# One head's row maxima among the last projections, and VectorE's subtractions at the streams' ends, in a two-layer attention trunk

## The chip, the core and the metric

The kernel runs on one core of one Trainium2 chip. The metric is the device time of one execution in microseconds (us); three runs of the kernel before took 2885.28 to 2890.05 us, with a median of 2886.47 us. TensorE (PE in the profile) multiplies, VectorE (DVE), ScalarE (ACT) and GpSimd (POOL) work on elements, SyncE (SP) issues most loads and stores.

## The reference

The function maps `x` (2048 x 1024, fp32) to an output of the same shape through two layers. Each layer is, in short:

```
hn   = rms_norm(h, norm_pre[i])
proj = hn @ w_in                      # q, k, v (or low-rank parts of them), memory queries, gate
main = 12 causal heads of width 64    # layer A: latent attention with rotary keys
                                      # layer B: logits plus F[t] - F[s], F the cumulative log forget gate
mem_out = 4 heads of cross-attention into 256 memory tokens
y    = concat(main, mem_out) * silu(gate)
h    = h + rms_norm(y @ w_out[i], norm_post[i])
```

Every product is computed at about fp32 precision: an operand is split into a high and a low part, and three products of parts are summed.

## The kernel before

**Stages.** Each layer has projections (layer A: `proj_a`, `up_a`; layer B: `proj_b`, L870 on), an attention stream and `out_proj`. Layer A's `out_proj` and layer B's projections run interleaved. Queries are taken in four groups of 512 (`g`), keys in blocks of 128.

**The stream.** A `Unit` is one head and one group g; a memory unit is one memory head and one group. The stream goes through the units in steps of up to 1024 columns (`flow`): logits on PE (`s_logits`, L1709), exponential on ACT (L1651), its fp16 high part on ACT (`hi`, L202), the low part, exponential minus high part (`lo`, L224), on POOL where the step is wider than 512 columns and else on DVE, then the values on PE (L1725). Before a unit's first step its rows must be there: the maxima of its logits, which PE computes (L1580 for causal units, L1562 for memory units), DVE reduces (L1551; L1583 for the masked block on the diagonal) and PE and DVE write as extra rows beside q (L1600, L1601). In the steady stream the rows of later units stand between the steps of earlier ones.

**The start of layer B's stream.** The last chunk of the projections is run for g = 1, 2, 3, 0. Before g = 3, `att_start` records the memory head, with eight early memory units whole (`run_early`: rows, logits, values) at a higher priority, so that they come between projection matmuls; before g = 0, `att_head` records the loads of head 0's keys and values. Head 0's rows stand at the head of the stream itself.

**q tiles.** A causal unit of layer B needs a q tile of 76 rows (`qb`, four per head, even heads in slot A3, odd ones in A0) and one of 128 rows (`qa`). Of the second kind there are four in slot R1, and four more in another slot (A4) for units after the last memory unit and a few more (`free`).

**out_proj.** For an output tile t of 128 queries, `z_prep` loads the gate and the attention output (L1195, L1196), multiplies them on POOL (L1200), transposes on PE (L1204), and splits; the matmuls are L1229. `z_prep(0)` is recorded behind the loads of two gains.

**What sets the order.** The projections and the early units are ordered by a scheduler with priorities; in the streams every engine follows the order in which the code records, SP too. The buffers are tiles in named slots (A0 to A8, R0 to R4, S, G, Q), which are given out again when their last reader is done, and a load into a slot waits for that on SP with all that is queued behind it.

Of the kernel before, what the change touches and what calls it, by code (L numbers as in the profile page):

```python
# [42 lines left out]
NR = 4  # L43
# [9 lines left out]
MEM_EARLY = {0: 6, 1: 8}  # L53
MEM_FIRST = {0: 4, 1: 4}
# [138 lines left out]
class Trunk:  # L193
    def __init__(self, tc, ins, out):
        self.tc, self.nc, self.i, self.out = tc, tc.nc, ins, out
        self.alt = 0
        self.owed = 0.0

# [663 lines left out]
    def proj_b(self, hn0):  # L862
# [153 lines left out]

    def att_start(self, l):

        nc, B = self.nc, self.box
        if l == 0:  # L1020
# [15 lines left out]
        ap["pm"], ap["ps"], ap["pv"] = self.banks(2, 3), self.banks(5, 6), self.banks(0)  # L1036
        self.l, self.yt = l, {}
# [28 lines left out]
    def att_head(self):  # L1066

        l, B = self.l, self.box
        self.v0 = B("A2" if l == 0 else "A8")
        self.kv_place("0", B("A1" if l == 0 else "A2", r=True), self.v0)  # L1070
# [3 lines left out]
        for _, f, _ in self.head0.prep():  # L1074
            f()

    def attention(self):
        nc, l, ap, B = self.nc, self.l, self.ap, self.box
        nb = DH + FB
# [5 lines left out]
        mb, jb = (v0, yb) if l == 0 else (ap["sp"],) * 2  # L1085
        mqk = self.mqk = mb.tile([P, G], BF16, name="mqk")
        ap["mj"] = Turn(jb.tile([P, G], BF16, name="mj"))
        nc.gpsimd.memset(mqk, 0.0)
        nc.gpsimd.affine_select(out=mqk[:, G - P:G], in_=mqk[:, G - P:G], compare_op=ALU.is_ge, fill=NEG, base=0,
                                pattern=[[-1, P]], channel_multiplier=1)  # L1090
# [5 lines left out]
        if l:  # L1096
            qa = B("R1", r=True)
            ap["qa"] = Turn(*(Later(lambda k=k: qa.tile([P, G], F32R, name=f"qa{k}")) for k in range(4)))
            qb = B("A3", r=True), B("A0", r=True)
            self.qb_t = [qb[j // NG].tile([nb, 2, G], F32R, name=f"qb{j}") for j in range(2 * NG)]  # L1100
            for g in range(NG):
# [693 lines left out]
```

## Time and profile before

| what | value |
|---|---|
| median of 3 runs | 2886.47 us |
| profiled execution, its own time | 2885.39 us |
| its span (first to last instruction) | 2883.7 us |
| PE busy, mean granted clock | 2789.8 us (97%), 0.976 |
| DVE, ACT, POOL busy | 1563.8, 1323.0, 1251.2 us |

The shares are means over stages. The places at which PE is not at its full clock and busy are what the tables below are cut from: the start and the end of each stream, and two short waits within the second one. A granted clock of 1.00 is 2.4 GHz and 0.50 is 1.2 GHz.

### The profile page before, as it was taken

What the parts mean: (1) busy time and instruction counts of PE and PEld (TensorE: products, weight loads), DVE (VectorE), ACT (ScalarE), POOL (GpSimd) and SP (SyncE); (2) the same over time, 40 slices, a digit from 0 to 9 for tenths busy, and PEclk for the clock granted to TensorE, in tenths of its full rate; (3) what the DMA queues carried; (4) which work ended last, traced back from release to release, by engine and by line L of the source; (5) the groups of instructions that cost most, each with busy time, mean ns of one, the idle gap of its engine ahead of it and who ended that gap; (6) DMA issues with size and microseconds to landing.
All of it is one profiled execution on the core that took longest, in us unless ns stands there. A gap on an engine that the chain in (4) does not pass through costs nothing. (4 is left out here: it accounts for less than half of the span.)

```text
span 2883.7 us, 58600 instructions
## 1 busy us (share of the span) xinstructions
PE 2789.8 (97%) x24017; PEld 2379.9 (83%) x24017; DVE 1563.8 (54%) x3358; ACT 1323.0 (46%) x1867; POOL 1251.2 (43%) x838
## 2 busy tenths in 40 slices
PE   7999999879999999999999999999999999999998
PEld 6789998657888888878888997999767788887787
DVE  7522215467777777745463325310268788887343
ACT  4322123237778788852141010111137788888311
POOL 2110123346677777772101002310037788888431
PEclk9999999979999999999999999999979999999999
DMA  5343447763433343255443223861454454465453
GB/s 186 125 140 100 133 146 264 229 204 93 106 74 88 76 100 93 55 190 190 146 156 118 76 82 121 291 225 61 132 149 113 116 134 123 112 171 170 147 175 117
DMA packets 260933, 398.42 MB, mean 138 GB/s; under 512 B 24793, under 2 KB 140521, under 8 KB 260521
## 3 DMA queue, kind: packets, MB, share of 16 engines
q1 hardware_dynamic: 180112, 255.21, 31.4%
q10 hardware_dynamic: 79016, 138.27, 13.3%
q8 instruction: 189, 3.10, 0.5%
q0 software_dynamic: 1536, 1.18, 0.3%
q14 instruction: 80, 0.65, 0.1%
HBM read 238.13 MB, written 156.47 MB: 137 GB/s over the span
## 5 line engine op out<-in xcount | busy, mean ns | idle before, releaser
L224 POOL TENSOR_TENSOR bA<-bA,bA 128x1024 f16<-128x1024 f32 (+5 forms) x277 | 507.8, 1844 | 293.9 <-ACT bA L202 219.5
L255 PE MATMUL banks<-bR,bA 128*128 128x256 f32 (+3 forms) x4437 | 549.1, 286 | 1.1 <-DVE bQ L507 0.6
L255 PEld LDWEIGHTS banks<-bR,bA 128*128 128x128 f32 x4437 | 540.7, 188 | 6.5 <-ACT bG L505 0.9
L255 PE MATMUL banks<-bA,bR 128*128 128x512 f32 (+2 forms) x2208 | 514.6, 390 | 6.9 <-ACT bS L823 4.2
L1709 PE MATMUL banks<-bA,bA 96*128 96x512 f32 (+13 forms) x1820 | 483.9, 377 | 0.3 <-ACT bA L1651 0.2
L255 PEld LDWEIGHTS banks<-bA,bR 128*128 128x128 f32 x2208 | 403.4, 191 | 93.3 <-ACT bS L823 5.4
L1651 ACT ACTIVATE bA<-banks 128x1024 f32<-128x1024 f32 (+1 forms) x414 | 370.7, 895 | 182.9 <-PE banks L1709 156.9
L1551 DVE TENSOR_REDUCE mx<-banks 128x1 f32<-128x512 f32 x576 | 387.8, 685 | 108.3 <-PE banks L1580 105.6
L202 ACT ACTIVATE bA<-bA 128x1024 f16<-128x1024 f32 (+5 forms) x400 | 336.5, 848 | 95.8 <-DMA qrs<-bA 22.0
L1709 PEld LDWEIGHTS banks<-bA,bA 96*128 96x128 f32 (+3 forms) x1820 | 327.5, 193 | 43.1 <-ACT bA L1651 0.9
L1580 PE MATMUL banks<-bA,bA 76*128 76x512 f32 (+5 forms) x868 | 317.3, 406 | 17.6 <-DVE bA L1601 4.9
L209 POOL TENSOR_SCALAR bR<-bR 128x1024 fp32r<-128x1024 f32 (+3 forms) x50 | 61.5, 1230 | 410.8 <-PE banks L255 360.1
L1583 DVE CUSTOM_DVE_ANT_0 bA<-banks,bA 128x128 bf16<-128x128 f32 (+3 forms) x384 | 186.6, 486 | 76.7 <-PE banks L1580 66.1
L1229 PE MATMUL banks<-bA,bA 128*128 128x512 f32 x960 | 226.6, 392 | 0.0
L1725 PEld LDWEIGHTS <-bA 128*128 128x128 f16 x5928 | 198.9, 99 | 28.9 <-issue 16.5
L1229 PEld LDWEIGHTS banks<-bA,bA 128*128 128x128 f32 x960 | 178.6, 188 | 36.1
L1580 PEld LDWEIGHTS banks<-bA,bA 76*128 76x128 f32 (+1 forms) x868 | 164.2, 196 | 50.5 <-DVE bA L1601 7.6
L1709 PE MATMUL banks<-bR,bA 128*128 128x512 f32 (+6 forms) x620 | 201.6, 391 | 0.9 <-DVE bR L1601 0.9
L224 POOL TENSOR_TENSOR bR<-bR,bR 128x1024 f16<-128x1024 f32 (+2 forms) x74 | 159.9, 2161 | 81.7 <-ACT bR L202 49.5
L1200 POOL TENSOR_TENSOR bA<-bA 128x512 f32<-128x512 f32 x64 | 102.4, 1622 | 207.8 <-DMA bA<-gs 195.1
L224 POOL TENSOR_TENSOR bR<-bA,bR 128x1024 f16<-128x1024 f32 (+2 forms) x76 | 154.7, 2038 | 67.4 <-ACT bR L202 31.0
L505 ACT ACTIVATE bG<-banks 128x256 f32<-128x256 f32 x128 | 49.1, 385 | 277.2 <-PE banks L255 197.2
(228 smaller groups left out, 3638.7 us busy)
## 6 DMA issues: line engine op xcount, KB each, us to landing
bA<-qbs SPq DMA_DIRECT2D x65, 256.0 KB
bA<-in_x_dram SPq DMA_DIRECT2D x32, 512.0 KB
gs<-bG ACTq DMA_DIRECT2D x128, 128.0 KB
bA<-gs SPq DMA_DIRECT2D x32, 512.0 KB
bA<-ys SPq DMA_DIRECT2D x32, 512.0 KB
bA<-h SPq DMA_DIRECT2D x28, 512.0 KB
ks<-bA ACTq DMA_DIRECT2D x24, 512.0 KB
qs<-bA ACTq DMA_DIRECT2D x24, 512.0 KB
```

The costliest lines, as they stand in the source:

```text
L202: nc.scalar.activation(out, in_, AF.Copy, scale=scale)
L209: nc.gpsimd.tensor_scalar(out, in_, scale, 0.0, op0=ALU.mult, op1=ALU.add)
L224: e.tensor_tensor(out=out, in0=in_, in1=hi, op=ALU.subtract)
L255: nc.tensor.matmul(out, lhsT=a, rhs=b, start=start and i == 0, stop=stop and i == n - 1)
L1200: nc.gpsimd.tensor_tensor(out=gt[:, hs], in0=gt[:, hs], in1=yt[:, hs], op=ALU.mult)
L1229: nc.tensor.matmul(ps[:, ns], lhsT=a, rhs=b[:, ns], start=c == 0 and j == 0, stop=c == KC - 1 and j == 2)
L1551: nc.vector.tensor_reduce(out=to, in_=ps, axis=AX.X, op=ALU.max, negate=negate)
L1580: nc.tensor.matmul(ps, lhsT=q[0:qr, t * P:(t + 1) * P], rhs=k[0:kr, x:x + w], start=True, stop=True)
L1583: nc.vector.tensor_tensor_reduce(out=ap["mj"].next()[:, 0:w], in0=ps, in1=K.mqk[:, G - w:G], scale=1.0, scalar=-3.0e38, op0=ALU.add, op1=A ...
L1651: nc.scalar.activation(pf[:, 0:w], ps[:, 0:w], AF.Exp, scale=self.scale, bias=LOGP)
L1709: nc.tensor.matmul(ps[:, o:o + bw], lhsT=k[0:kr, (self.k0 + kt) * P:(self.k0 + kt + 1) * P], rhs=q[0:qr, q0:q0 + bw], start=i == 0 and not ...
L1725: nc.tensor.matmul(self.pv[:, t, 0:n], lhsT=p[:, o:o + P], rhs=v[:, kv, a:a + n], start=self.first, stop=False, skip_group_check=True)
```

## The change

Layer B's first causal head and its memory units change places. `att_head` is called before the chunk g = 2, takes head 0's slots (k in A4, v in A5, q rows in A6) and now also records the row maxima of all four of head 0's units, at a priority of its own; `att_start` follows before g = 0. Four early memory units are run whole instead of eight, two more get only their rows (`ready`), and two instead of four stand ahead of head 0 in the stream; further memory units stand behind two groups of each head from head 0 on, so that they last for five heads. The planner counts rows that are there already, and q tiles are loaded ahead at each step. The slots of layer B move: the `qb` tiles of even heads are in A6 and those of odd heads in A3, late `qa` tiles in A7. When all rows of a stream are recorded, `lo` runs on DVE at every width, right behind the step's ACT work. In `out_proj` the first two output tiles are multiplied on DVE, and `z_prep(0)` is recorded ahead of the gains.

```diff
-MEM_EARLY = {0: 6, 1: 8}
-MEM_FIRST = {0: 4, 1: 4}
+ROWS_AHEAD = 600
+MEM_EARLY = {0: 6, 1: 4}
+MEM_READY = {0: 2, 1: 2}
+MEM_FIRST = {0: 4, 1: 2}
...
-            if g == 0:
+            if g == 2:
                 yield
-            elif g == 3:
+                env = (stp, self.banks(4, 7), hn)
+            elif g == 0:
                 yield
-                env = (stp, self.banks(4, 7, 1), hn)
             for k, (_, ms) in enumerate(last):
                 self.run_chunk(env, ms, W[len(jobs) - 2 + k], g)
...
-            km, ph, pa, ymp, qq = B("A4", r=True), B("A5"), B("A7"), B("A1"), B("R4", r=True)
+            km, ph, pa, ymp, qq = B("A7", r=True), B("A1"), B("A2"), B("A8"), B("R4", r=True)
             pl, pfs, vmp, vrp, nrp, sp, qqs = ph, (pa,) * 3, ymp, ymp, pa, pa, (km, km, qq, qq)
...
-        for u in first:
+        ready = self.mem_units[:MEM_READY[l]]
+        for u in first + ready:
             u.q = ap["qq"].next()
         with self.tc.high_priority(offset=EARLY_AHEAD):
-            run_early(mem, first)
+            run_early(mem, first, ready)
 
     def k_ones(self, j):
         k = self.k_t[j]
...
+        self.att_place(l)
+        self.v0 = B("A2" if l == 0 else "A5")
+        self.kv_place("0", B("A1" if l == 0 else "A4", r=True), self.v0)
...
+        self.ready = {}
+        if l == 0:
+            return
+        self.max_mask(self.v0, self.v0)
+        self.qb_t = {}
+        self.qb_place("A6", 0)
+        with self.tc.high_priority(offset=ROWS_AHEAD):
+            for g in range(NG):
+                u = self.ready[g] = Unit(self, l, self.head0, 0, g)
+                u.q_row()
+                for f, _ in u.max_closures():
+                    f()
+                u.nm()
+                u.nm_row()
+
...
+    def qb_place(self, slot, odd):
+
+        nb = DH + FB
+        box = self.box(slot, r=True)
+        for g in range(NG):
+            t = self.qb_t[g + NG * odd] = box.tile([nb, 2, G], F32R, name=f"qb{g}")
+            ind = self.v0.tile([FB, G], F32, name="ind")
+            self.nc.gpsimd.memset(ind, 1.0)
+            for lo_b, hi_b in ((-(NR + 2 * g), 0), (0, NR + 1 + 2 * g)):
+                self.nc.gpsimd.affine_select(out=ind, in_=ind, compare_op=ALU.is_ge, fill=0.0, base=lo_b + hi_b,
+                                             pattern=[[0, G]], channel_multiplier=1 if lo_b else -1)
+            self.nc.vector.tensor_copy(t[DH:nb], ind[:, None, :].to_broadcast([nb - DH, 2, G]))
...
-        self.kv_place("1", B("A3" if l == 0 else "A6", r=True), yb if l == 0 else B("Q"))
+        self.kv_place("1", B("A3" if l == 0 else "A0", r=True), yb if l == 0 else B("Q"))
...
         units = [mu.pop(0) for _ in range(min(MEM_FIRST[l], len(mu)))]
         for h, hd in enumerate(heads):
...
-            late = mid + [later("A4", q1, k) for k in range(4)]
+            late = mid + [later("A7", q1, k) for k in range(4)]
...
-            u.q = min(ts, key=lambda q: used.get(q, -1))
+            u.q = u.q or min(ts, key=lambda q: used.get(q, -1))
...
-        zb, gb, xp = (B("A1", r=True), B("A2"), B("A8")) if l == 0 else (B("A1", r=True), B("A3"), B("A4"))
+        zb, gb, xp = (B("A1", r=True), B("A2"), B("A8")) if l == 0 else (B("A8", r=True), B("A3"), B("A7"))
         sp = self.sm
         pt_, po, npt = self.banks(2, 3), self.banks(4, 6), self.banks(0, 1)
-        gain = xp.tile([P, D], F32, name="ogain")
-        self.bcast_row(gain, i["norm_post"][l])
-        if l == 0:
-            self.xbox = B("A6")
-            gpre = self.gpre = self.xbox.tile([P, D], F32, name="ogpre")
-            self.bcast_row(gpre, i["norm_pre"][1])
-
...
-                nc.gpsimd.tensor_tensor(out=gt[:, hs], in0=gt[:, hs], in1=yt[:, hs], op=ALU.mult)
+                (nc.vector if t < 2 else nc.gpsimd).tensor_tensor(out=gt[:, hs], in0=gt[:, hs], in1=yt[:, hs], op=ALU.mult)
...
         nxt = z_prep(0)
+        gain = xp.tile([P, D], F32, name="ogain")
+        self.bcast_row(gain, i["norm_post"][l])
+        if l == 0:
+            self.xbox = B("A6")
+            gpre = self.gpre = self.xbox.tile([P, D], F32, name="ogpre")
+            self.bcast_row(gpre, i["norm_pre"][1])
...
-    for u in objs[:3]:
+    both = objs + ready
+    for u in both[:3]:
         u.q_dma()
-    for u in objs[:2]:
+    for u in both[:2]:
         rows(u)
     for k, u in enumerate(objs):
-        if k + 3 < len(objs):
-            objs[k + 3].q_dma()
-        if k + 2 < len(objs):
-            rows(objs[k + 2])
+        if k + 3 < len(both):
+            both[k + 3].q_dma()
+        if k + 2 < len(both):
+            rows(both[k + 2])
...
+        if o.has_row:
+            at += sum(c for _, c in o.max_closures())
+            maxq.extend(late)
+            late.clear()
+            continue
...
+        q_ahead(u + 2, u)
         close()
-        todo = advance(u, min(t * rate + lead, RUNUP * (t + 4 * G) + need[0]))
+        todo = advance(u, min(t * rate + lead, RUNUP * (t + 4 * G) + need[0] + done))
...
-        o.flow(s, box)
+        o.flow(s, box, st["k"] == len(maxq) and not todo)
         if before:
             before[0].flow_lo(before[1])
         before = None
+        if st["k"] == len(maxq) and not todo:
+            o.flow_lo(box)
+            box["dve"] = False
...
+    def q_row(self):
+
+        K, h, g = self.K, self.h, self.g
+        if self.mx_ops:
+            return
+        kb, nb = self.hd.kt[1], DH + FB
+        qb = self.qb = K.qb_t[g + NG * (h % 2)]
+        K.load_r(qb[0:DH], K.qbs[h // 2][(h % 2) * DH:(h % 2) * DH + DH, :, g * G:(g + 1) * G])
+        self.mx_ops = ((qb[:, 0], nb), (kb, nb))
+        self.nmrow, self.at = qb[DH:DH + NR, 1], DH
...
+        if self.loaded:
+            return
+        self.loaded = True
         if self.kind == "fox":
-            src = K.qbs[h // 2][r, :, sl]
+            self.q_row()
...
-            K.load_r(qa, src[:, 0].unsqueeze(0).to_broadcast([2, DH, G]))
-            self.mx_ops = ((qb[:, 0], nb), (kb, nb))
-            self.nmrow, self.at = qb[DH:DH + NR, 1], DH
-            self.passes = [((ka, P), (qa, P)), ((kb, nb), (qb[:, 1], nb))]
+            K.load_r(qa, K.qbs[h // 2][r, 0, sl].unsqueeze(0).to_broadcast([2, DH, G]))
+            self.passes = [((ka, P), (qa, P)), ((kb, DH + FB), (self.qb[:, 1], DH + FB))]
...
-        if w > G:
+        box["dve"] = w <= G or last
+        if not box["dve"]:
             K.lo("pool", pl[:, 0:w], pf[:, 0:w], ph[:, 0:w])
 
     def flow_lo(self, box):
         w = box["w"]
-        if w <= G:
+        if box["dve"]:
             self.K.lo("dve", box["pl"][:, 0:w], box["pf"][:, 0:w], box["ph"][:, 0:w])
...
     next(pb)
+    K.att_head(1)
+    next(pb)
     K.att_start(1)
-    next(pb)
-    K.att_head()
     drain(pb)
```

**At the end of layer B's projections, on PE.** `banks_64` is PSUM, L255 (L258 in the changed kernel) is a projection, L1562, L1600, L1709 belong to memory units. Before:

```order
L1562 MATMUL banks_64<-bA4_21125,bR4_21129 128x256 x2
L1709 MATMUL banks_64<-bR4_21129,bA4_21125 128x512 x2
L255 MATMUL banks_64<-bA3_14575,bR0_16016 128x512
L255 MATMUL banks_64<-bA3_14575,bR3_16015 128x512
L255 MATMUL banks_64<-bA0_14576,bR3_16015 128x512
L255 MATMUL banks_64<-bA3_14575,bR0_16016 128x512
L1562 MATMUL banks_64<-bA4_21125 128x256 x2
L1709 MATMUL banks_64<-bR4_21129,bA4_21125 128x512
L1600 MATMUL banks_64<-idr_73,nmw_82 68x128
L1562 MATMUL banks_64<-bA4_21125 128x256 x2
L1709 MATMUL banks_64<-bR4_21129,bA4_21125 128x512 x3
```

After the change (L1630 is a row matmul of head 0, L1612 of a memory unit, L1650 writes rows):

```order
L258 MATMUL banks_64<-bA3_14575,bR3_16015 128x512
L258 MATMUL banks_64<-bA0_14576,bR3_16015 128x512
L258 MATMUL banks_64<-bA3_14575,bR0_16016 128x512
L1630 MATMUL banks_64<-bA4_21018,bA6_21036 128x512
L1630 MATMUL banks_64<-bA4_21018,bA6_21036 128x256
L1630 MATMUL banks_64<-bA4_21018,bA6_21036 128x512 x6
L1630 MATMUL banks_64<-bA4_21018,bA6_21036 128x384
L1630 MATMUL banks_64<-bA4_21018,bA6_21036 128x512
L1612 MATMUL banks_64<-bA7_21369 128x256 x6
L1650 MATMUL banks_64<-idr_73,nmw_82 68x128
L1612 MATMUL banks_64<-bA7_21369 128x256 x2
```

The last projection matmuls had rows and logits of memory units between them, and head 0's first row matmul came 110 rows of the order later; now they have head 0's row matmuls between them, ten of these (one row counts six) and all memory rows follow.

**Within layer B's stream, on SP.** `qbs1` are q rows of heads 2 and 3, R1 and A4 (A7 after the change) are slots of 128-row `qa` tiles, `vsp` values, `qms1` memory queries, `kbs` keys, `frd` rows of the forget gate. Before:

```order
L1465 DMA bQ_21743<-vsp_139 128x520 x2
L1014 DMA bA0_21751<-qbs1_125 64x2x512
L1014 DMA bR1_21749<-qbs1_125 128x1x512
L1014 DMA bA0_21751<-qbs1_125 64x2x512
L1014 DMA bA4_23915<-qbs1_125 128x1x512
L1465 DMA bQ_21743<-vsp_139 128x520
L1014 DMA bA3_21750<-qbs2_126 64x2x512
L1014 DMA bA4_23915<-qbs2_126 128x1x512
L1014 DMA bA3_21750<-qbs2_126 64x2x512
```

After the change:

```order
L1506 DMA bQ_21696<-vsp_139 128x520 x2
L1017 DMA bA3_21699<-qbs1_125 64x2x512
L1017 DMA bR1_21698<-qbs1_125 128x1x512
L1017 DMA bA3_21699<-qbs1_125 64x2x512
L1017 DMA bR1_21698<-qbs1_125 128x1x512
L1017 DMA bA7_21369<-qms1_1_143 64x2x512
L1017 DMA bA7_21369<-qms1_1_143 64x512
L1017 DMA bA4_21018<-frd_136 12x2048
L1017 DMA bA4_21018<-kbs2_132 64x2x512
L1017 DMA bA4_21018<-kbs2_132 64x512
L1017 DMA bA6_21036<-qbs2_126 64x2x512
L1017 DMA bR1_21698<-qbs2_126 128x1x512
```

In the order before, the fourth group of head 3 already takes a tile of the further slot; in the order after, the fourth group of head 3 and the first of head 4 stay with the four tiles of R1, and memory queries are loaded between them. The first `qa` tile of A7 is loaded later, with `qbs3` (heads 6 and 7).

**At the end of layer B's stream, on SP.** `ws` are output weights, `gs` and `ys` the gate and the attention output (a load into A3, or a store of `ys`). Before:

```order
L1195 DMA bA3_30436<-gs1_145 128x1024 x2
L1742 DMA ys1_151<-bR0_21741 128x4x128
L1014 DMA bA2_29976<-ws_152 128x1024 x4
L1196 DMA bA3_30436<-ys1_151 128x1024 x2
L1742 DMA ys1_151<-bR0_21741 128x4x128
L1014 DMA bA8_30045<-ws_152 128x1024 x4
L1196 DMA bA3_30436<-ys1_151 128x1024
L1195 DMA bA3_30436<-gs1_145 128x1024
L1196 DMA bA3_30436<-ys1_151 128x1024
L1742 DMA ys1_151<-bR0_21741 128x4x128
L1196 DMA bA3_30436<-ys1_151 128x1024
L328 DMA bA4_30437<-in_norm_post_dram 128x1024
```

After the change:

```order
L1793 DMA ys1_151<-bR0_21694 128x4x128
L1017 DMA bA4_29980<-ws_152 128x1024 x4
L1793 DMA ys1_151<-bR0_21694 128x4x128
L1017 DMA bA5_30049<-ws_152 128x1024 x4
L331 DMA bA7_30441<-in_norm_post_dram 128x1024
L1249 DMA bA7_30441<-h1_0_153 128x1024
L1793 DMA ys1_151<-bR0_21694 128x4x128
L1218 DMA bA3_30440<-gs1_145 128x1024
L1219 DMA bA3_30440<-ys1_151 128x1024
L1218 DMA bA3_30440<-gs1_145 128x1024
L1219 DMA bA3_30440<-ys1_151 128x1024 x2
```

The gate of the first output tile was loaded ahead of the last weights; now it stands behind them, behind the gain and the residual, and behind a store, and its slot A3 holds odd heads' q rows until the last step's logits.

## Rows read from the trace of the kernel before

**Rows 1.** The page: its first line, and PE's busy time.
```profile
span 2883.7 us, 58600 instructions
PE 2789.8 (97%) x24017; PEld 2379.9 (83%) x24017; DVE 1563.8 (54%) x3358; ACT 1323.0 (46%) x1867; POOL 1251.2 (43%) x838
```

**Rows 2.** Windows around the second stream's start: length; busy us (count) by engine; clock; DMA.
```profile
2124.00:2184.00 60.00, 53.89 (x387) 39.17 (x387) 49.49 (x106) 27.18 (x31) 27.07 (x21) 0.69 0.52 129
2136.00:2148.00 12.00, 8.70 (x42) 5.77 (x41) 11.41 (x22) 2.08 (x2) 5.97 (x7) 0.50 0.48 126
```

**Rows 3.** Timeline of PE, last projection matmuls: start, us, line, operation.
```profile
2126.82 1.10 PE L255 MATMUL banks<-bA,bR 128*128 128x512 f32 x4
```

**Rows 4.** Groups by form, DVE alone, 2126 to 2170: count, busy us, mean ns, idle before.
```profile
L1108 DVE CAST bA<-bA 12x1024 fp32r<-12x1024 f32 x8 | 7.2, 940 | 0.6 <-PE banks L255 0.6
L1551 DVE TENSOR_REDUCE nmw<-banks 128x2 fp32r<-128x512 f32 x11 | 7.2, 680 | 1.5 <-PE banks L1562 1.4
L1601 DVE TENSOR_TENSOR bA<-banks,spread 4x512 fp32r<-4x512 f32 x4 | 2.8, 689 | 0.1
L224 DVE TENSOR_TENSOR bA<-bA,bA 128x512 f16<-128x512 f32 x2 | 1.5, 771 | 0.0
```

**Rows 5.** Groups by form, 2400 to 2600, the steady second stream.
```profile
L224 POOL TENSOR_TENSOR bA<-bA,bA 128x1024 f16<-128x1024 f32 x63 | 134.1, 2143 | 22.4 <-ACT bA L202 9.5 <-issue 7.5 <-DVE mx L1551 2.9
L202 ACT ACTIVATE bA<-bA 128x1024 f16<-128x1024 f32 x79 | 83.6, 1058 | 2.6
L1651 ACT ACTIVATE bA<-banks 128x1024 f32<-128x1024 f32 x79 | 80.5, 1019 | 20.3 <-PE banks L1709 15.4 <-PE banks L1600 2.5 <-POOL bA L224 1.4
```

**Rows 6.** Timeline of PE, two waits for q rows of the second stream.
```profile
2241.67 0.47 PE L1580 MATMUL banks<-bA,bA 76*128 76x512 f32 x1 [1.43 <-DMA bA<-qbs]
...
2287.22 1.40 PE L1580 MATMUL banks<-bA,bA 76*128 76x512 f32 x3 [2.62 <-DMA bA<-qbs]
```

**Rows 7.** Windows around these two waits.
```profile
2240.00:2248.00 8.00, 6.57 (x68) 5.64 (x67) 4.56 (x13) 3.66 (x5) 3.92 (x2) 0.79 0.50 137
2284.00:2294.00 10.00, 7.38 (x66) 5.80 (x65) 4.25 (x12) 4.20 (x5) 5.29 (x4) 0.66 0.50 131
```

**Rows 8.** Timeline of several engines, the second stream's end.
```profile
2653.88 1.01 ACT L1651 ACTIVATE bA<-banks 128x1024 f32<-128x1024 f32 x1
...
2659.29 2.51 POOL L1200 TENSOR_TENSOR bA<-bA 128x512 f32<-128x512 f32 x2 [0.94 <-DMA bA<-ys]
...
2686.49 1.17 PE L1229 MATMUL banks<-bR,bA 128*128 128x512 f32 x4
...
2688.37 1.07 PE L1204 MATMUL banks<-idf,bA 128*128 128x128 f32 x8
2689.20 1.17 PE L1229 MATMUL banks<-bR,bA 128*128 128x512 f32 x4
```

**Rows 9.** Waits of PE, 2652 to 2690: us in total, times, longest.
```profile
PE banks L1725 <- POOL bA L224: 5.0, 3, 2.2
```

**Rows 10.** Groups by form, DVE over the whole span.
```profile
L224 DVE TENSOR_TENSOR bA<-bA,bA 128x256 f16<-128x256 f32 x46 | 59.8, 1301 | 17.6 <-ACT bA L202 16.0
L224 DVE TENSOR_TENSOR bR<-bR,bR 128x1024 fp32r<-128x1024 f32 x32 | 39.8, 1247 | 129.5 <-POOL bR L209 125.0 <-PE banks L1229 4.4
```

**Rows 11.** Waits of PE, 1250 to 1264, the first stream's end.
```profile
PE banks L1204 <- POOL bA L1200: 1.8, 2, 1.2
PE banks L1725 <- DVE bR L224: 1.0, 1, 1.0
PE banks L1725 <- POOL bR L224: 0.8, 1, 0.8
```

**Rows 12.** Timeline of SP and POOL there.
```profile
1254.21 0.38 SPq L1196 DMA_DIRECT2D bA<-ys  x1
...
1259.08 2.48 POOL L1200 TENSOR_TENSOR bA<-bA 128x512 f32<-128x512 f32 x2 [1.29 <-DMA bA<-ys]
```

**Rows 13.** Waits of PE, 600 to 660, the first stream's start.
```profile
PE banks L1562 <- DMA bA<-qms: 5.6, 3, 3.6
```

More of the change, by code (lines that the diff above doesn't have):

```diff
@@ L1075, in att_head, with max_mask @@
             f()
+        self.ready = {}
[12 more added lines that the diff above has]
+                u.nm_row()
+    def max_mask(self, mb, jb):
+        mqk = self.mqk = mb.tile([P, G], BF16, name="mqk")
+        self.ap["mj"] = Turn(jb.tile([P, G], BF16, name="mj"))
+        self.nc.gpsimd.memset(mqk, 0.0)
+        self.nc.gpsimd.affine_select(out=mqk[:, G - P:G], in_=mqk[:, G - P:G], compare_op=ALU.is_ge, fill=NEG, base=0,
+                                     pattern=[[-1, P]], channel_multiplier=1)
@@ L1084, in attention @@
         gb, fewer = B("G"), None
[L1085 to L1090, printed above, removed]
+        if l == 0:
+            self.max_mask(v0, yb)
         more = (v0, yb, gb, ap["sp"]) if l == 0 else (ap["ymp"], gb, v0, v0)
@@ L1098, in attention @@
             ap["qa"] = Turn(*(Later(lambda k=k: qa.tile([P, G], F32R, name=f"qa{k}")) for k in range(4)))
-            qb = B("A3", r=True), B("A0", r=True)
-            self.qb_t = [qb[j // NG].tile([nb, 2, G], F32R, name=f"qb{j}") for j in range(2 * NG)]
-            for g in range(NG):
-                ind = v0.tile([FB, G], F32, name="ind")
-                nc.gpsimd.memset(ind, 1.0)
-                for lo_b, hi_b in ((-(NR + 2 * g), 0), (0, NR + 1 + 2 * g)):
-                    nc.gpsimd.affine_select(out=ind, in_=ind, compare_op=ALU.is_ge, fill=0.0, base=lo_b + hi_b,
-                                            pattern=[[0, G]], channel_multiplier=1 if lo_b else -1)
-                for j in (g, g + NG):
-                    nc.vector.tensor_copy(self.qb_t[j][DH:nb], ind[:, None, :].to_broadcast([nb - DH, 2, G]))
+            self.qb_place("A3", 1)
         heads = [self.head0] + [Head(self, l, "mla" if l == 0 else "fox", h) for h in range(1, HEADS)]
@@ L1113, in attention @@
             for g in range(NG):
-                units.append(Unit(self, l, hd, hd.h, g))
+                units.append(self.ready[g] if h == 0 and self.ready else Unit(self, l, hd, hd.h, g))
                 if g in MEM_AFTER[l] and mu:
@@ L1255, in out_proj, with run_early @@
                 yield
-def run_early(mem, objs):
+def run_early(mem, objs, ready):
     K = mem.K
@@ L1307, in run_units @@
         late.append((u, o.nm_row, 0))
-    maxq.append(late.pop())
+    maxq.extend(late)
     steps = [(u, s, max(b[1] + b[3] for b in s)) for u, o in enumerate(objs) for s in o.steps()]
-    need = [0] * n
-    for u, f, c in maxq:
-        need[u] += c
+    cur = [1] * n
+    for u, o in enumerate(objs):
+        cur[u] = o.hd.idx or cur[max(u, 1) - 1]
+    need = [sum(c for _, c in o.max_closures()) for o in objs]
     width = [0] * n
@@ L1315, in run_units @@
         width[u] += w
+    done = sum(need[u] for u, o in enumerate(objs) if o.has_row)
     rate = sum(need) / sum(width)
@@ L1336, in run_units @@
     aux.sort(key=lambda x: (x[0], x[1]))
-    st = dict(k=0, done=0, dma=0)
+    st = dict(k=0, dma=0)
     def run_aux(t, head=-1):
@@ L1360, in advance @@
             u, f, c = maxq[st["k"]]
-            if u > main and not (st["done"] + c <= target and u <= main + AHEAD):
+            if objs[u].hd.idx > cur[main] + 1 or u > main and not (c <= target and u <= main + AHEAD):
                 break
@@ L1367, in advance @@
             todo.append(f)
-            st["done"] += c
             st["k"] += 1
@@ L1639, in main_closures, with flow @@
         return out
-    def flow(self, blocks, box):
+    def flow(self, blocks, box, last):
         K, nc, ap = self.K, self.K.nc, self.K.ap
```

36 lines of the change are left out of this document (18 added, 18 removed).

## The prediction

> **What bounds the kernel now.** I read the page first: PE is busy for 2789.8 of 2883.7 us [rows 1], so only the stretches where PE idles or runs below its full clock can give anything back, and DVE, ACT and POOL matter where PE waits for them. The windows show the start of the second stream as the largest of these: from 2124 to 2184 us PE is busy 53.89 of 60 us at a mean clock of 0.69 [rows 2]. Busy time times clock is the work at full clock, 37.2 us, so 22.8 us are lost there. One window of it has PE at 0.50, which is its 1.2 GHz level, and DVE busy 11.41 of 12 us: DVE bounds it. The last projection matmuls end near 2127.9 [rows 3]; what follows is head 0's row maxima, which DVE reduces. Next come two waits of PE for q rows, 1.43 and 2.62 us [rows 6]; by their windows they cost 8 − 6.57 × 0.79 = 2.8 us and 10 − 7.38 × 0.66 = 5.1 us [rows 7], since the clock falls to the lower level for a while after each. At the second stream's end PE waits three times, 5.0 us in all, for POOL's low parts [rows 9], because POOL puts `out_proj`'s products between them, two for 2.51 us [rows 8]. The first stream's end has 3.6 us of such waits [rows 11], its start 5.6 us for memory queries [rows 13].
>
> A profiled execution of 2885.39 us is what the sum is made against: 1.7 us more than the span, 1.1 us less than the median. I add 1.1 us at the end. What a measurement can tell from no change is 0.2%, 5.8 us.
>
> **The start of the second stream.** The change moves reductions, it removes none: the matmuls are the same in number and form. Before, memory units filled the last projections and head 0's 40 row matmuls came after; now 30 of the 40 are among the projections, 10 and the memory units after them. So I count DVE's work behind the last projection in the new order, with durations of before: 7 reductions of causal rows and 14 of memory rows at 0.68, 3 casts of forget-gate rows at 0.94, 8 row writes at 0.689, 4 low parts at 0.771 [rows 4]: 14.3 + 2.8 + 5.5 + 3.1 = 25.7 us, and four outputs of memory units of some 0.6 us each, an estimate from the row writes, make 28. PE's work in that phase is 57 matmuls of up to 512 columns and 96 narrow ones. Four matmuls of 512 columns took 1.17 us from start to end [rows 8], about 0.24 us each from start to start; with narrow ones as small, this is about 15 us. So the phase is DVE's again, 28 to 33 us with the gaps of a ping-pong between the two engines, and loses 13 to 18 us. Then eight steps without rows between them follow, and there POOL's low part, 2.143 us, and ACT's exponential and high part, 1.019 + 1.058 = 2.08 us [rows 5], are both longer than PE's work of about 1.8 us a step: 2 to 3 us lost, and about 1 us for the two `ready` units' queries, which wait for slots of earlier ones. In all 15 to 22 us instead of 22.8; I take 18.8, since the row nearest to the case, the DVE-bound window, has PE at its lower level throughout. That is 4 us gained, between 1 and 8.
>
> **q tiles within the stream.** The memory units now last for five heads, so the stage with four 128-row q tiles lasts to head 6; before, the fourth group of head 3 left it. The two waits of [rows 6] fall in that stage: a load of a q tile waits on SP until the tile four units earlier has had its last logits, the rows' own q load is queued behind it, and PE waits for that. The SP order of heads 2 to 5 after the change has the pattern that heads 2 and 3 had when they waited. The earlier loading at every step (`q_ahead`) issues an instruction sooner in SP's order, but a slot that isn't free holds it anyway. Two more such waits at the mean of 2.8 and 5.1 us are 8 us lost. From nothing (the memory units between make the waits shorter) to three at the larger price, 15 us.
>
> **The second stream's end.** From the last step's rows on, the steps left are ten full ones and two of 256 columns. Without POOL, ACT bounds them: 2653.88 [rows 8] plus 10 × 2.08 plus 2 × 0.8, estimated from a quarter of the columns and the fixed part, gives 2676.3; the low parts on DVE at about 1.25 us [rows 10] fit below ACT's 2.08. The last low part and values end near 2678. But the first output tile's gate now waits on SP for A3, which the last logits read, near 2674.5. At the first stream's end the later of two such loads was issued at 1254.21 and the product started at 1259.08, 4.9 us later [rows 12]. By that the product starts near 2679.4, and product (0.69, as DVE's other passes over 512 columns [rows 4]), transposes, ACT's and DVE's split (some 2 us) put the first output matmul at about 2682. Before, the steady output matmuls begin at 2689.20, with four already done at 2686.49 and the second tile's transposes at 2688.37 [rows 8], which is worth about 2 us: 2687.3. Gain about 4.5 us, from 1 (the loads take 8 us behind the gain and the residual) to 9 (they are hidden).
> Where DVE and POOL work side by side a DVE low part is slow: the 256-column ones took 1.30 us on average, more than a 1024-column pass at 1.247 [rows 10]. The page GPSIMD Engine Reference of the Trainium skill (Specifications) says that GpSimd's access to the on-chip memory is shared with VectorE and contends when VectorE reads two inputs there, which these low parts do; by it the first two low parts on DVE, beside POOL's last two, would take longer and the gain would be some 2 us less. The trace agrees that they slow each other; how a 1024-column one fares beside POOL, no run shows so far.
>
> **The first stream's end and start.** The 3.6 us of waits [rows 11] are for POOL's low parts and products and for a DVE low part beside POOL. Their work goes to DVE, which is idle there, but `ys` lands at about 1259.08 as before [rows 12]: product, transposes and split then follow sooner by half of POOL's 2.48 us and a little. I take 2 us, from 0.5 to 3.3. At the start the queries of two memory units are asked for earlier, and head 0's loads remain where they were: 0.5 us, from −2 to 3 [rows 13].
>
> **Sum.** 4 − 8 + 4.5 + 2 + 0.5 = 3 us faster: 2885.4 − 3 = 2882.4, with 1.1 about 2883.5 us.
>
> **The rivals.**
> *The reductions really are hidden.* If PE keeps its full clock through the last projections and the DVE phase falls to 28 us without gaps and the later steps lose nothing, the start loses some 12 us instead of 22.8, 10 to 11 gained; with no more waits for q tiles, 4.5 + 2 + 0.5 come on top, 17 to 18 us in all: 2869. For it speaks that POOL and ACT have room before the stream; against it that DVE has the same work in one stretch. With half of it the time is about 2877.
> *The four q tiles decide.* If each of heads 2 to 5 has its wait at the price of the worse one, 5.1 us [rows 7], four against two before, at 2.8 and 5.1, are 12.5 us more; if the start gains nothing besides, because the memory rows now stand alone behind the projections, and the output tile's late load eats the gain of the end, the time is 2885.4 + 12.5 − 2.5 + 1.1, about 2896.5. It decides from the point at which the waits cost more than the 11 us that the ends and the start give: three further waits at 4 us.
> *The end doesn't change.* The words "first output tile first" don't hold in layer B: the order on SP has the gain, the residual and a store ahead of its gate. If the loads take 8 us from 2674.5, the output begins where it did, and the time is 2888.
>
> **How the numbers follow.** The forecast case, between 2879 and 2888, has 0.40; the first rival, whole or in half, 0.30, the second 0.20, the third 0.10. The forecast case is 0.12 faster by over 0.2% (its lower end lies below 2880.7), else the same; the first rival is nearly all faster (0.29 of 0.30); the second has 0.16 slower and 0.04 the same; the third 0.08 the same and 0.02 slower. So faster 0.41, same 0.41, slower 0.18. The range leaves out one in ten at either side: 2869 to 2896; the forecast case's own is 2879 to 2888.
>
> **What the profile after would show.** The start: head 0's row matmuls (the causal line) before the last projections, DVE busy 90% and more for about 28 us behind them, and PE's lost time from there to the first causal rows of head 1 at 15 to 22 us instead of 22.8. The q tiles: about four waits of PE for `qbs` in heads 2 to 5, each with a window at a clock of 0.7 to 0.8. The end: no POOL low parts after the last row, ACT without gaps, then 2 to 4 us of PE waiting for the product whose releaser is the load of `ys`. I am wrong if PE waits for `qbs` no more than before (then faster), if the stretch behind the projections loses under 13 us (faster), or if the output matmuls start as late as before (slower).

## The result: slower by 0.7%, and the profile after

Five runs of the changed kernel took 2902.07 to 2917.11 us, median 2904.47, beside 2885.28 for five runs of the kernel before: ratio 1.0073, 95% interval 1.0056 to 1.009. 2883.5 us and a range of 2869 to 2896 us were predicted; the time lies above it. The profiled execution is the slowest of the five (2917.11 us), so the stretches below add up to about 32 us where the median has 19. Its page:

```profile
span 2915.4 us, 58611 instructions
...
PE 2812.0 (96%) x24017; PEld 2398.7 (82%) x24017; DVE 1584.4 (54%) x3380; ACT 1323.6 (45%) x1863; POOL 1212.5 (42%) x824
```

To find where time goes, I cut both traces at events that both have: the end of the last projection matmuls, the first row matmul of head 1, a row write of head 8 in the steady stream, the last row write, the end. Windows of the changed kernel, columns as in [rows 2]:

```profile
2115.40:2176.40 61.00, 52.60 (x399) 36.42 (x398) 37.58 (x67) 33.05 (x39) 31.86 (x23) 0.69 0.37 95
2176.40:2530.20 353.80, 337.61 (x4117) 274.56 (x4117) 258.54 (x588) 270.85 (x300) 258.87 (x123) 0.91 0.44 114
```

and of the kernel before, same events:

```profile
2127.90:2189.60 61.70, 55.59 (x422) 40.69 (x422) 52.20 (x113) 30.26 (x33) 31.64 (x23) 0.70 0.52 129
2189.60:2495.66 306.06, 297.67 (x3919) 243.14 (x3918) 244.72 (x559) 257.96 (x288) 246.51 (x117) 0.98 0.46 121
```

Length minus busy time times clock is what a stretch loses. The start loses 61.0 − 52.6 × 0.69 = 24.7 us, where it lost 22.8. The stream from head 1 to the steady part loses 353.8 − 337.6 × 0.91 = 46.6 us, where it lost 14.3: this is nearly the whole loss, 32 us (a hundredth of the clock is 3 us here). Of these 32 us, PE's idle time is 8, from 8.4 to 16.2; the rest is time at its lower clock. From the last row to the end it took 230.1 us before and takes 227.4 (2915.4 − 2688.04).

Within the stream PE's waits, columns as in [rows 9], show one entry that grew; before there were two such waits, 4.1 us in all [rows 6]:

```profile
PE banks L1630 <- DMA bA<-qbs: 13.4, 7, 2.5
```

Four of the seven in the timeline of PE, to be read beside [rows 6]:

```profile
2176.40 1.23 PE L1630 MATMUL banks<-bA,bA 76*128 76x128 f32 x4 [0.94 <-DMA bA<-qbs]
...
2182.44 0.77 PE L1630 MATMUL banks<-bA,bA 76*128 76x512 f32 x1 [2.48 <-DMA bA<-qbs]
...
2237.28 0.76 PE L1630 MATMUL banks<-bA,bA 76*128 76x512 f32 x1 [2.28 <-DMA bA<-qbs]
...
2345.61 0.77 PE L1630 MATMUL banks<-bA,bA 76*128 76x512 f32 x1 [1.37 <-DMA bA<-qbs]
```

The seven are of two kinds. Two stand at head 1's first rows (2176.40 and 2182.44), where the kernel before had none; the other five come once per head in heads 2 to 6, the longer stage of four q tiles. The first two have a price of their own. The 23.6 us behind head 1's first row lose 23.6 − 20.99 × 0.64 = 10.2 us in the changed kernel (first line) and 1.3 us before (second line); the rest of the stream to head 8, with the five waits, loses some 36 us instead of 13.

```profile
2176.40:2200.00 23.60, 20.99 (x175) 16.84 (x176) 11.39 (x31) 10.76 (x13) 10.96 (x6) 0.64 0.32 94
2189.60:2213.20 23.60, 22.30 (x299) 18.13 (x298) 17.53 (x43) 19.10 (x20) 18.45 (x9) 1.00 0.28 77
```

Head 1's first loads are late because a store ahead of them on SP waits for VectorE (waits of SP from 2140 to 2166 in the changed kernel; total, times, longest):

```profile
SPq L1793 <- DVE bA L1789: 14.6, 1, 14.6
```

SP in front of the wait at 2345.61 (start, length, operation): two key loads took 5.82 us to issue, and the q rows' load went out at 2340.85, 4.8 us before PE could go on:

```profile
2333.82 5.82 SPq L1017 DMA_DIRECT2D bA<-kbs  x2
...
2340.85 0.52 SPq L1017 DMA_DIRECT2D bA<-qbs  x1
```

What SP waited for from 2170 to 2470 (total, times, longest): with four tiles it stands (it waits, and every load behind it waits too), for PE or for a load into R1 still under way. In the kernel before these two entries are 62.5 and 18.1 us.

```profile
SPq L1017 <- PE banks L1630: 92.2, 15, 19.0
...
SPq L1017 <- DMA bR<-qbs: 29.2, 9, 5.4
```

At the start, DVE is busy for 20 of the first 24 us, where 90% and more for about 28 us were forecast. From 2136 to 2148 PE itself is busy throughout, at its lower level:

```profile
2112.00:2124.00 12.00, 8.59 (x28) 5.15 (x26) 10.04 (x19) 1.88 (x2) 3.45 (x6) 0.84 0.29 111
2124.00:2136.00 12.00, 10.14 (x26) 5.99 (x25) 9.95 (x17) 3.84 (x6) 3.38 (x4) 0.50 0.11 27
2136.00:2148.00 12.00, 12.00 (x93) 9.13 (x92) 8.21 (x16) 4.95 (x7) 4.57 (x3) 0.50 0.36 93
2148.00:2160.00 12.00, 10.28 (x64) 7.38 (x64) 3.91 (x8) 7.22 (x9) 5.89 (x4) 0.64 0.17 54
```

The end, several engines (last row, first low part on DVE, the gate's load, product, transposes, output matmuls):

```profile
2688.04 0.28 PE L1650 MATMUL banks<-idr,nmw 128*68 128x128 f32 x1 [0.43 <-DVE nmw L1643]
...
2692.58 1.30 DVE L227 TENSOR_TENSOR bA<-bA,bA 128x1024 f16<-128x1024 f32 x1 [2.60 <-ACT bA L205]
...
2703.20 2.27 PE L1776 MATMUL banks<-bQ,bA 128*128 128x65 f16 x48 [1.75 <-DVE bR L1789]
...
2710.47 0.32 SPq L1218 DMA_DIRECT2D bA<-gs  x1
...
2710.85 0.42 SPq L1219 DMA_DIRECT2D bA<-ys  x1
...
2715.48 1.29 DVE L1223 TENSOR_TENSOR bA<-bA 128x512 f32<-128x512 f32 x2 [1.04 <-DMA bA<-ys]
2716.23 1.26 PE L1227 MATMUL banks<-idf,bA 128*128 128x128 f32 x8 [2.01 <-DVE bA L1223]
...
2717.57 5.72 PE L1258 MATMUL banks<-bR,bA 128*128 128x512 f32 x17
```

The gate's load stands at 2710.47, behind the last logits, and PE waits 2.01 us for the product whose own wait is for `ys`. At 2703.20 there is a wait that was not forecast: a division of DVE (L1789) stands behind low parts that wait for ACT, and PE waits 1.75 us for it.

The first stream's end, SP, DVE and PE:

```profile
1254.93 0.38 SPq L1219 DMA_DIRECT2D bA<-ys  x1
...
1259.71 1.29 DVE L1223 TENSOR_TENSOR bA<-bA 128x512 f32<-128x512 f32 x2 [2.36 <-DMA bA<-ys]
1260.46 1.97 PE L1227 MATMUL banks<-idf,bA 128*128 128x128 f32 x8 [1.98 <-DVE bA L1223]
...
1262.27 1.96 PE L1258 MATMUL banks<-bA,bA 128*128 128x512 f32 x5
```

Output matmuls start at 1262.27; before, the first was at 1262.03, with the product begun at 1259.08 [rows 12].

### The profile page after: what moved, and what is told of

Same layout as the page of the kernel before. It is cut to its first block, busy times and chain, and to the rows that moved or that the text cites. A ratio compares the mean times of both kernels' runs of the same rounds, so it can differ in the third digit from the quotient of the medians.

```text
span 2915.4 us, 58611 instructions
## 1 busy us (share of the span) xinstructions
PE 2812.0 (96%) x24017; PEld 2398.7 (82%) x24017; DVE 1584.4 (54%) x3380; ACT 1323.6 (45%) x1863; POOL 1212.5 (42%) x824
## 4 chain that ended last, share of the span: by engine, by line
PE 72%; DMA 11%; issue 8%; DVE 5%; POOL 1%; ACT 1%; ACTq 0%; SPq 0%; DVEq 0%; POOLq 0%
PE banks L258 24%; PE banks L1760 16%; PE banks L1258 12%; PE banks L1776 10%; PE banks L1630 7%; DMA bA<-qbs 1%; DMA qs<-bA 1%; DMA bR<-qbs 1%; PE banks L1227 1%; DMA ws<-bA 1%; PE banks L349 1%; DMA bA<-vs 1%; DMA bR<-in_w_in_b_dram 1%; DMA vsp<-bA 1%; DMA ys<-bR 1%
## 5 line engine op out<-in xcount | busy, mean ns | idle before, releaser
L227 POOL TENSOR_TENSOR bA<-bA,bA 128x1024 f16<-128x1024 f32 (+5 forms) x269 | 492.7, 1842 | 279.5 <-ACT bA L205 204.3
L258 PE MATMUL banks<-bR,bA 128*128 128x256 f32 (+3 forms) x4437 | 549.5, 286 | 2.3 <-ACT bG L508 1.7
L258 PEld LDWEIGHTS banks<-bR,bA 128*128 128x128 f32 x4437 | 540.8, 188 | 7.9 <-ACT bG L508 2.3
L258 PE MATMUL banks<-bA,bR 128*128 128x512 f32 (+2 forms) x2208 | 513.4, 388 | 7.3 <-ACT bS L826 4.4
L1760 PE MATMUL banks<-bA,bA 96*128 96x512 f32 (+6 forms) x1764 | 478.7, 379 | 0.0
L258 PEld LDWEIGHTS banks<-bA,bR 128*128 128x128 f32 x2208 | 401.5, 190 | 92.3 <-ACT bS L826 4.9
L1760 PEld LDWEIGHTS banks<-bA,bA 96*128 96x128 f32 (+3 forms) x1764 | 321.4, 195 | 41.1
L1630 PE MATMUL banks<-bA,bA 76*128 76x512 f32 (+5 forms) x868 | 323.6, 410 | 30.2 <-DMA bA<-qbs 13.4
L1760 PE MATMUL banks<-bR,bA 128*128 128x512 f32 (+11 forms) x676 | 227.5, 398 | 2.0 <-ACT bA L1701 1.9
L1776 PEld LDWEIGHTS <-bA 128*128 128x128 f16 x5932 | 205.5, 101 | 25.0 <-issue 18.9
L1630 PEld LDWEIGHTS banks<-bA,bA 76*128 76x128 f32 (+1 forms) x868 | 167.2, 198 | 64.0 <-issue 17.1
L227 POOL TENSOR_TENSOR bR<-bR,bR 128x1024 f16<-128x1024 f32 (+2 forms) x71 | 153.6, 2164 | 84.6 <-ACT bR L205 38.1
L1223 POOL TENSOR_TENSOR bA<-bA 128x512 f32<-128x512 f32 x56 | 91.9, 1663 | 227.3 <-DMA bA<-gs 191.4
L227 POOL TENSOR_TENSOR bR<-bA,bR 128x1024 f16<-128x1024 f32 (+2 forms) x73 | 148.7, 2039 | 69.8 <-ACT bR L205 33.8
```

Of the source, the lines that this page charges most:

```text
L227: e.tensor_tensor(out=out, in0=in_, in1=hi, op=ALU.subtract)
L258: nc.tensor.matmul(out, lhsT=a, rhs=b, start=start and i == 0, stop=stop and i == n - 1)
L1223: (nc.vector if t < 2 else nc.gpsimd).tensor_tensor(out=gt[:, hs], in0=gt[:, hs], in1=yt[:, hs], op=ALU.mult)
L1630: nc.tensor.matmul(ps, lhsT=q[0:qr, t * P:(t + 1) * P], rhs=k[0:kr, x:x + w], start=True, stop=True)
L1760: nc.tensor.matmul(ps[:, o:o + bw], lhsT=k[0:kr, (self.k0 + kt) * P:(self.k0 + kt + 1) * P], rhs=q[0:qr, q0:q0 + bw], start=i == 0 and not ...
L1776: nc.tensor.matmul(self.pv[:, t, 0:n], lhsT=p[:, o:o + P], rhs=v[:, kv, a:a + n], start=self.first, stop=False, skip_group_check=True)
```

## The experiments

Theory 1: the stage with four 128-row q tiles, longer now, makes PE wait for q rows. Theory 2: the memory units, spread over five heads, do it by their own loads and rows.

**e1: more q tiles in the changed kernel.**

```diff
-early, mid = few + [later(x, q2, k) for x in ("R2", "R3") for k in range(2)], ap["qa"].tiles
-late = mid + [later("A7", q1, k) for k in range(4)]
+early, mid = few + [later("R3", q2, k) for k in range(2)], ap["qa"].tiles + [later("R2", q1, k) for k in range(4)]
+late = ap["qa"].tiles + [later("A7", q1, k) for k in range(4)]
```

> The changed kernel with four more 128-row q tiles, in slot R2, for the stage in which it has four in R1 (memory queries lose R2's two tiles and keep R3's). Theory 1, the four q tiles: in the changed kernel PE waits seven times for q rows (13.4 us) between the first rows of head 1 and the steady stream, and loses 45 us there by busy time and clock, 13 before. With eight tiles at most two such waits are left, that stretch loses 13 to 20 us, and the time is 2872 to 2888 us. Theory 2, the memory units themselves: their loads and rows, now spread over five heads, crowd SP's queue and the rows, whatever q tiles there are. Then at least five waits for q rows are left and the time stays at 2898 to 2910 us.

Measured: 2886.81 us, ratio to the kernel before 0.9996 (0.9982 to 1.0011). PE's waits, and SP's in the same stretch:

```profile
PE banks L1630 <- DMA bA<-qbs: 2.9, 2, 1.9
```

```profile
SPq L1017 <- PE banks L1630: 39.5, 8, 10.9
...
SPq L1017 <- DMA bR<-qbs: 4.7, 6, 1.3
```

Two waits instead of seven, and SP waits 5 us for R1 instead of 29. The two that are left are those at head 1's first rows, at 2176.91 and 2182.75; the five of heads 2 to 6 are gone. Theory 1 holds: with the tiles 18 of the 19 us come back. They also take away the two waits that the kernel before had (7 us, the step from e4 to e5), so the equal time doesn't say that nothing else is lost.

**e2: the longer stage in the kernel before, and nothing else.**

```diff
-free = max([k for k, u in enumerate(units) if u.kind == "mem"], default=0) + AHEAD + 2
+free = max([k for k, u in enumerate(units) if u.kind == "mem"], default=0) + AHEAD + 2 + 12 * l
```

> The kernel before, with only the stage of four q tiles made longer by twelve units, to the head where the changed kernel ends it; memory units, slots and all else as before. Theory 1 (four q tiles): three to five more waits for q rows than the two before, at 3 to 5 us each: 2895 to 2910 us. Theory 2 (memory units spread over the heads): nothing changes, 2883 to 2889 us.

Measured: 2906.28 us, ratio 1.0056 (1.0036 to 1.0076). The stage's length alone gives a loss of this size, with memory units where they were; SP waits 99.1 and 34.7 us from 2170 to 2470, much as in the changed kernel. Theory 2 falls.

```profile
PE banks L1580 <- DMA bA<-qbs: 13.4, 6, 3.3
```

**e3: the gate in A6.**

```diff
-B("A8", r=True), B("A3"), B("A7")
+B("A8", r=True), B("A6"), B("A7")
```

> The changed kernel with out_proj's gate and attention tiles of layer B in A6 (q rows of even heads, free after head 10) instead of A3 (odd heads, free after the last logits). Theory: the first tile's loads are issued before the last weights again, PE's wait of 2.0 us for the product goes, and with it the issue at 2710 behind the last logits: 2 to 5 us less than the changed kernel, 2899 to 2903 us, and the wait for q rows is untouched. Rival: the last ys store and ACT's chain bound the end, and nothing is gained: within 1.5 us of the changed kernel in the stretch from the last row to the end.

Measured: 2909.13 us (2904.21 to 2913.82), ratio to the kernel before 1.007 (1.0047 to 1.0094): above the 2899 to 2903 us of the theory, and within the scatter of the changed kernel, so the time doesn't tell. In the one profile the stretch from the last row to the end is 223.65 us against 227.4, and PE's wait for the product is shorter:

```profile
PE banks L1227 <- DVE bA L1223: 0.8, 1, 0.8
```

**e4: the ends alone, on the kernel before.** The three edits of the diff at the streams' ends (`last` in `flow`, the products of t < 2 on DVE, `z_prep(0)` first), slots as before.

> The kernel before, with only the edits at the streams' ends: low parts on VectorE once all rows are recorded, the first two products on VectorE, first product ahead of the gains; its slots as before, so that the gate's loads stay early. Theory: the three waits for POOL (5.0 us) and the half clock behind them go, and the second stream's end gains 5 to 8 us, the first one's loses or gains under 1: 2877 to 2881 us. Rival: ACT's exponentials bound the end and DVE's finish of a unit stands behind low parts, so that the gain is what the changed kernel has there, 3 us: 2882 to 2884 us.

Measured: 2879.1 us, ratio 0.9974 (0.9959 to 0.9989). From the last row to the end 225.5 us, 4.6 less than before; the median fell by 7.4, as the theory had it, and where the rest lies stays open. Two waits are left there:

```profile
PE banks L1728 <- DVE bR L1741: 2.9, 1, 2.9
PE banks L1197 <- DVE bA L1193: 1.0, 1, 1.0
```

**e5: e4 with e1's tiles.**

> The kernel before with the edits at the streams' ends (2879.1 us by itself) and with four more 128-row q tiles in R2 for the stage that has four. Theory (four tiles make the waits): the two waits for q rows of the kernel before, 2.8 and 5.1 us by busy time and clock, shrink to at most one small one, and 3 to 8 us go: 2871 to 2876 us. Rival: the waits stand where rows of several units are loaded at once, whatever tiles there are, as two are left in the changed kernel with eight tiles: 2878 to 2881 us.

Measured: 2871.74 us (2869.4 to 2875.58), ratio 0.9947 (0.9931 to 0.9962), faster than both kernels. No wait for q rows is left; the longest entries of PE from 2170 to 2500:

```profile
PE banks L1582 <- DVE bA L1603: 2.9, 8, 0.4
PE banks L1602 <- DVE nmw L1553: 1.0, 1, 1.0
PE banks L1582 <- DVE mx L1553: 0.9, 2, 0.5
```

At its end PE waits 2.8 us for DVE's division, as in e4 (2.9 us), and the trace shows one reason. POOL begins the product of the third output tile just before a DVE low part of 1024 columns, which then takes 2.23 us (2.33 in e4) instead of the 1.23 us that it takes alone, and the division stands behind it:

```profile
2660.17 1.23 DVE L224 TENSOR_TENSOR bA<-bA,bA 128x1024 f16<-128x1024 f32 x1 [1.25 <-ACT bA L202]
2662.01 3.47 POOL L1193 TENSOR_TENSOR bA<-bA 128x512 f32<-128x512 f32 x2 [10.22 <-DMA bA<-gs]
2662.12 2.23 DVE L224 TENSOR_TENSOR bA<-bA,bA 128x1024 f16<-128x1024 f32 x1 [0.73 <-ACT bA L202]
...
2664.48 0.48 DVE L1741 SCALAR_TENSOR_TENSOR bR<-banks,vsc,r 128x256 f32<-128x256 f32 x1
```

**e6: e1 and e3 together.**

> The changed kernel with eight q tiles in the early stage and with the gate's tiles in A6. If the two act at different places and add, this is 2886.8 less some 2 to 4 us, 2882 to 2885 us, and beside the kernel before with the ends alone (2879.1 us) it says what is left as the price of the new start of the second stream: 3 to 6 us. Rival: the new start is itself a gain of 3 to 4 us, as was forecast: then it is below 2878 us.

Measured: 2885.88 us, ratio 0.9986 (0.997 to 1.0001). The edits at A6 add little that shows, and the rival falls: the new start is no gain. 14 us lie between e5 and e6, but not all of them are the start's price. In the profiles the stretch from the last projection to about 24 us behind head 1's first row loses 31 us in e6 (24.0 and 6.9 by busy time and clock) and 25 to 26 in e5; the rest lies elsewhere and no run separates it.

**e7 and e11: the load of rows' q apart from the four tiles.** e7 records it up to two units ahead:

```diff
+for v in range(st["dma"], min(upto + 1, n)):
+    if objs[v].kind == "fox":
+        objs[v].q_row()
...
-if st["dma"] <= u:
+if st["dma"] <= u and not objs[u].mx_ops:
```

e11 as soon as the slot is free in the plan, up to eight units ahead.

> The changed kernel with four q tiles as it is, but a unit's 76-row q tile (which its row maxima need, and of which there are eight) is loaded as soon as the plan comes near it, without waiting for a 128-row tile to come free in the plan. Theory 1a: the waits come from this coupling: a unit's rows' q is recorded for loading only when the unit four earlier has no steps left, so that the rows follow their load by less than the load's 5 us. Then the waits go with four tiles as with eight: at most two are left, 2878 to 2890 us. Theory 1b: SP stands at the load into the 128-row tile and the next rows' load behind it comes late anyway: then most of the seven waits stay, above 2897 us.

> The changed kernel with its four q tiles, with 76-row q tiles loaded as soon as their slot is free in the plan, up to eight units ahead, so that on SP they stand ahead of the next head's keys and of the loads into R1. Theory (order on SP: with four tiles a unit's row load comes to stand behind key loads and an R1 load that wait for PE): the waits for q rows fall to two or fewer and the time to 2880 to 2890 us, with four tiles. Rival (the tiles themselves: the rows can't be reached before the load into one of four tiles is done): five waits or more, 2897 to 2908 us.

Measured: e7 2903.19 us, ratio 1.0053 (1.0033 to 1.0074); e11 2903.32 us, ratio 1.0039 (1.0021 to 1.0056). PE's waits in e7:

```profile
PE banks L1633 <- DMA bA<-qbs: 7.8, 6, 1.7
PE banks L1615 <- DMA bR<-qms: 2.6, 3, 1.2
```

and in e11, with SP's below:

```profile
PE banks L1622 <- DMA bR<-qms: 5.1, 3, 2.6
PE banks L1640 <- DMA bA<-kbs: 3.0, 1, 3.0
...
PE banks L1622 <- DMA bA<-qms: 1.1, 1, 1.1
```

```profile
SPq L1017 <- PE banks L1640: 82.7, 17, 14.2
SPq L1017 <- DMA bR<-qbs: 35.2, 9, 5.1
```

In e7 most of the waits stay, as theory 1b had it. In e11 not one wait for q rows is left, as its theory had it, and the time is where its rival had it. The waits have gone over to memory queries and keys. SP stands in front of loads about as long as in the changed kernel (83 and 35 us); whichever load comes behind is late. That this standing bounds and the order only says who pays is the reading that fits, also with e2 (99 and 35 us) and e1 (40 and 5); standing in front of stores doesn't count in the same way, for e1's SP waits 71 us for DVE there. A part of the loss may have gone: beside the kernel before in their own series, e7 and e11 lose 16 and 13 us of the median, where the changed kernel lost 19.

**e8 and e10: low parts one step later.** On e4 and on e5:

```diff
-        if st["k"] == len(maxq) and not todo:
-            o.flow_lo(box)
-            box["dve"] = False
```

> The kernel before with the edits at the streams' ends, but a step's low part on VectorE is recorded one step later, as those of narrow steps are, and not right behind the step's ACT work. Theory: a finished unit's division on VectorE stood behind low parts that wait for ACT, and PE waited 2.9 us for it; one low part fewer stands ahead of it, the wait falls to about 1 us, and 1 to 2 us go from 2879.1. Rival: the values then wait for their low part one ACT step longer, 2 us per change of unit: 2879 to 2882 us.

> The kernel before with the ends' edits, eight q tiles (2871.7 us) and the low parts at the end one step later. In the trace of the kernel with that last edit the stretch from the last row to the end took 221.1 us instead of 225.5, but its time was not lower. Theory: the 4 us at the end are real and were hidden by the scatter of the waits for q rows, which are gone here: 2867 to 2870 us. Rival: nothing gained, 2871 to 2874 us.

Measured: e8 2880.29 us, ratio 0.9969 (0.9952 to 0.9985); e10 2871.16 us in only 4 runs, 0.9931 (0.9904 to 0.9959). In their profiles the end takes 221.1 and 221.6 us instead of 225.5 and 225.3, but neither time is lower by more than the scatter (2880.29 beside 2879.1 us, 2871.16 beside 2871.74). PE's wait for the division is gone in both. One profile each is against 4 to 10 runs; where the 4 us go stays open.

**e9: head 1's loads at the stream's start.** e6 with e11's edit, and

```diff
-aux.append((a + fr * (b - a), hd.idx if first else 97, f))
+aux.append((-1.0 if hd.idx == 2 and heads[0].K.ready else a + fr * (b - a), hd.idx if first else 97, f))
```

> The changed kernel with eight q tiles, the gate's tiles in A6 (2885.9 us so far), head 1's keys and values loaded at the start of layer B's stream and not along head 0's steps, and 76-row q tiles loaded when their slot is free in the plan. Theory: with eight tiles the second stream's start still loses about 30 us from 2110 to 2190 where the old start loses 24, because head 1's loads stand on SP behind a store that waits 13 us for VectorE, and PE waits twice for q rows (3.3 us and the half clock behind them). With the loads ahead these two waits go and 5 to 8 us with them: 2878 to 2881 us. Rival: the phase behind the projections is bounded by VectorE and what is not waited for q rows is waited for row maxima: 2884 to 2888 us.

Measured: 2880.08 us, ratio 0.9968 (0.9954 to 0.9982), 6 us less than e6, though the intervals of the two ratios overlap. The waits for q rows go, and one wait for memory queries comes, so that the stretch that lost 31 us in e6 still loses 28 to 30; most of the 6 us isn't seen there:

```profile
PE banks L1622 <- DMA bA<-qms: 4.5, 1, 4.5
PE banks L1640 <- DVE mx L1611: 3.0, 4, 1.0
```

## Why the prediction was wrong

**The q tiles: the right place and nearly the right count, too low a price.** The step "Two more such waits at the mean of 2.8 and 5.1 us are 8 us lost" failed. "About four waits" in heads 2 to 5 were forecast, and five came in heads 2 to 6, but they cost more: the stretch with them lost some 36 us instead of 13, about 23 more in the profiled execution, and e1 and e2 show 18 and 20 us of the median. The price was taken from two waits of before: in windows of 14 to 20 us around them the five lose 3.2 to 8.5 us each, 28 in all, and the two of before 8.6. The order gives which load is behind which, not how long SP stands. The step's range to 15 us was also drawn from these two waits, and its rival, with 12.5 us, was the nearest to the result. The description of the mechanism held: a load into R1 stands on SP and the next rows' load is queued behind it. That `q_ahead` would not help a slot that isn't free fits with e7 and e11, where earlier recording left SP's standing as it was; no run takes `q_ahead` out by itself.

**The start of the second stream: a loss, where 4 us of gain were forecast.** This is the second step that failed. To head 1's first row 18.8 us of loss were forecast and 22.8 became 24.7, and the 23.6 us behind it, which the step didn't count, lost 10.2 instead of 1.3: some 11 us lost in this slowest run, some 7 in e1 and e6. The bound of 15 to 22 us left out that head 1's loads stand on SP behind a store that waits 14.6 us for DVE, so that two of the seven waits for q rows fall here. DVE's phase was there, with 20 busy us in the first 24, but from 2136 to 2148 PE at its lower level was itself the limit. e9 takes the two waits away and is 6 us faster than e6, but a wait of 4.5 us for memory queries comes in their place; it stays 8 us above e5, which has the old start, so the 30 row matmuls among the projections bought nothing that these runs can show.

**The second stream's end: right in kind.** 4.5 us were forecast, 2.8 measured in the profile. The gate's load came behind the last logits, as forecast, and ACT bounded the steps. With the gate's load early, e4 gained 4.6 there. Missed was DVE's division behind the low parts, 1.75 us. The term for a DVE low part, about 1.25 us for 1024 columns, measured 1.23 alone; in the changed kernel the first one overlaps POOL's last for 0.2 us only and took 1.30, so the two hardly met. In e4 and e5 they did, and it took 2.33 and 2.23 us. What the Trainium skill's page GPSIMD Engine Reference (Specifications) says of contention with a VectorE instruction that reads two inputs agrees with these two; the 2 us that the prediction drew from it did not arise in the changed kernel.

**The first stream's end: no gain, where 2 us were forecast.** The load of `ys` was issued at 1254.93 and the product began at 1259.71, 0.6 us later than before. The step had named this load as its bound and assumed that it lands as before.

**The first stream's start: nothing, as forecast.** Its waits changed hands; the last row write of that stream is at 1232.3 and was at 1232.1. The waits for memory queries fell from 5.6 to 2.1 us, and PE now waits once, 6.7 us, before head 0's rows. The profile puts this wait down to a store; the loads of these q rows went out at 633.99, 4.7 us before PE went on, so they are the likelier cause (total, times, longest):

```profile
PE banks L1630 <- DMA ys<-bA: 6.7, 1, 6.7
```

The chances had slower at 0.18, and a range that ended at 2896; the term with the least evidence, two waits seen once, was the one that should have widened it upwards, and the start's term had no side on which the start loses.

## What to carry to other kernels

When a change makes a stage longer in which few buffers are given out in turn, price each turn of that stage and not the waits that were seen in it: in-order issue of loads turns one full buffer into a late load for whatever stands behind. If reordering the loads moves the wait to another name and leaves most of the loss, the issuing engine's standing is the likely bound, and another buffer is worth a trial: here it was the remedy (e1, e5). A gain at a stream's end can be had apart from the change it came with: e4 and e5 took what was good in this one.

## What was not expected of the hardware

A wait of 0.9 to 2.5 us cost more than itself: seven of them sum to 13.4 us, and the stretch lost 32 us more than before with two, because PE's clock fell to its lower level behind them (0.91 over the stretch instead of 0.98, and 0.64 in the 23.6 us behind the first).

A VectorE subtraction of 1024 columns that reads two inputs took 1.23 us alone and 2.23 to 2.33 us when a GpSimd product had begun just before it (e4, e5), and PE paid for it through the division that stood behind.

Whether waits for loads also make a kernel's time scatter stays open: e5, which has none for q rows, ran from 2869 to 2876 us and the changed kernel from 2902 to 2917, but e10, which has none either, spread over 11 us in four runs.
